# A hybrid decoder layer on one Trainium2 core: half 1's Q and T tables leave the input projection, scores change sign, key halves travel by DMA, and the down projection prepares three blocks ahead

## The chip, the cores and the metric

The kernel runs on one core of a Trainium2 chip. Its engines are TensorE (PE, with its weight loads PEld), VectorE (DVE), ScalarE (ACT), GpSimd (POOL) and SyncE (SP, which here only issues DMAs). The metric is the device time of one execution in microseconds, the median over several runs. One execution was profiled; all rows below are of that one.

## The reference

One decoder layer over 1024 tokens of width 1024. An input projection feeds two groups of heads: an S5 state-space group (32 channel groups of 16, each driving a 64-dimensional complex diagonal state) and a differential attention group (4 heads, two causal softmax maps each). Then an output projection, cross-attention over 256 memory tokens and a SwiGLU feed-forward, each with a residual and a LayerNorm. What the change touches:

```python
# S5: x_t = A x_{t-1} + B u_t, y = Re(C x) + D u, then gelu and a gate
_, _, xr, xi = lax.associative_scan(combine, (a_re, a_im, bu_re, bu_im), axis=1)
y = einsum(c_re, xr) - einsum(c_im, xi) + d * uf
y = gelu(y); y = y * sigmoid(y @ glu_w + glu_b)
...
# differential attention, per block of 128 queries
s = einsum('bqhd,bkhd->bhqk', qb, kb) * scale
s = where(dist >= 0, s + bias, -inf)
p = softmax(s, axis=-1)
attn = p[:, :, 0] - lam * p[:, :, 1]
...
# feed-forward
return (silu(gu[..., :FFN_HIDDEN]) * gu[..., FFN_HIDDEN:]) @ w_down
```

## The kernel before

**Numbers and matmuls.** All data is fp32. Most products are made as three matmuls of a rounded high part and a rest: a weight tile is loaded by SP (`wload`), then an engine rounds it (high) and subtracts (low). Where the engine is POOL, this is a TENSOR_SCALAR and a TENSOR_TENSOR of 128x1024, called a split below. Work tiles come from two pools: 47 slots `u` of 128x1024 and 6 slots `h` of 128x512. A tile takes the slot that has been free the longest, and waits until the last reader of that slot, which may be a DMA, is done. The profile drops the slot numbers: `u`, `h`, `sc`, `mm`, `tp` (the last three in PSUM) are families.

**Order.** The order on each engine is decided when the program is built: generators are woven by a planner with rough rates (`weave`), then the tile framework schedules. In the run it is fixed and each engine is in order.

**S5.** The scan runs in chunks of eight tokens. `s5_tables(hf)` builds, for half `hf` of the states, the tables in four steps: Q (DVE), T (POOL), the rotation table E (DVE) with the transposes of Q (PE, ACT), and short convolution rows `kr`: 32 matmuls, an ACT copy, a small DVE add, and DMA writes to DRAM on ACT's queue. `s5_quarter(q)` uses the tables of half `q // 2` for one quarter of the channels: SP loads the matrix M from `kr` (two DMAs), PE transposes the inputs (`Ut`) and makes v; DVE rotates v by E, runs two scans and rotates back (the rotation stage); PE sums Ut by M and the states by T; ACT and DVE make the gelu; PE transposes it; ACT writes it to DRAM (`yd`). `s5_pipe` staggers the four quarters. Beside the pipe PE has `fill`: value projection and the queries and keys of head 0.

In the kernel before, `u_proj` (the S5 input projection) is woven with `s5_tables(0)` and the first two steps of `s5_tables(1)`, Q and T; the pipe then runs the rest of `s5_tables(1)` at quarter 0.

**Attention.** `qk_proj(h + 1)` is woven with `attention(h)`. A query or key tile holds 64 channels; both 64-partition halves are filled, since the matmul takes 128 (for queries the other half holds the low part, for keys a copy). Per block and map, DVE adds the bias and takes the row maximum in one instruction, negates it (`nm`), and ACT takes the exponential with that bias.

**Down projection.** `prep(half, j)` loads block j of the weight and of the hidden activations (`hidd`, in DRAM) on SP's queue and makes high and low parts; `go` does the 24 matmuls of a block. One block is prepared ahead.

## Time and profile before

| | us |
|---|---|
| median of 3 runs (1537.68 to 1541.3) | 1539.12 |
| the profiled execution | 1539.39 |
| its span | 1537.6 |
| PE busy (share of the span) | 1424.8 (93%) |
| DVE busy | 937.7 (61%) |
| ACT busy | 528.5 (34%) |
| POOL busy | 476.7 (31%) |

The time of the profiled execution is 1.79 us longer than its span. PE is busy nearly throughout, so what a change is worth is to be looked for in the stretches where it isn't: around 120 to 200 us (the S5 pipe's start), in the attention from 280 to 480 us, and at single places later. The page also follows back the chain of work that ended last: PE 68%, DVE 13%, DMA 8%, POOL 4%, ACT 3%. All instructions are recorded under one helper line (L119, after the change L120), so rows are told apart by their tiles.

### The profile page before, as it was taken

The page shows a single profiled execution, that of the slowest core. Times are in us where ns is not written, and L with a number is a line of the kernel's source. Part 1 is how long each engine was busy: PE and PEld are TensorE (multiplying, and loading weights), DVE is VectorE, ACT ScalarE, POOL GpSimd, SP SyncE. Part 2 cuts the span into 40 slices and gives each one's busy share as a digit, 9 for nine tenths or more (in the row PEclk, how much of TensorE's full clock was granted, in tenths as well). Part 3 has the DMA queues.
Part 4 walks back from the last instruction along what each step waited for, and adds up shares of the span by engine and source line. Part 5 has one row for each costly group of instructions (what it writes and reads, how often), then busy time and mean ns, then how long its engine had stood idle before and what let it go on. Part 6 is the DMA issues. An engine that isn't in the chain of part 4 may idle for free.

```text
span 1537.6 us, 18794 instructions
## 1 busy us (share of the span) xinstructions
PE 1424.8 (93%) x7246; PEld 1202.6 (78%) x7246; DVE 937.7 (61%) x1603; ACT 528.5 (34%) x926; POOL 476.7 (31%) x382
## 2 busy tenths in 40 slices
PE   7985699999796999999999899999999998999996
PEld 6985588878676788888787677878888887888885
DVE  8893667766796555635547856656655547237405
ACT  5411233645684012424212632323323325233300
POOL 4354121022004766000155645534444420003102
PEclk9998799999998899999999999999999999999998
DMA  9104531100346224123322223322222248554501
GB/s 341 68 1 83 96 97 56 42 28 5 105 134 231 74 83 137 56 69 124 110 83 82 96 84 116 108 77 82 90 82 82 83 153 305 165 165 172 183 28 55
DMA packets 52333, 162.61 MB, mean 106 GB/s; under 512 B 5834, under 2 KB 10351, under 8 KB 52244
## 3 DMA queue, kind: packets, MB, share of 16 engines
q1 hardware_dynamic: 41652, 124.17, 24.7%
q0 software_dynamic: 7696, 26.74, 4.7%
q10 hardware_dynamic: 2896, 10.51, 2.9%
q8 instruction: 57, 0.93, 0.3%
q14 instruction: 32, 0.26, 0.1%
HBM read 126.77 MB, written 34.62 MB: 105 GB/s over the span
## 4 chain that ended last, share of the span: by engine, by line
PE 68%; DVE 13%; DMA 8%; POOL 4%; ACT 3%; issue 3%; ACTq 1%; SPq 0%; POOLq 0%; DVEq 0%
PE mm L119 35%; PE sc L119 27%; DVE u L119 9%; PE tp L119 7%; POOL u L119 3%; ACT u L119 3%; DMA u<-in_wdown_dram 1%; DMA u<-in_wgu_dram 1%; DMA u<-in_wqk_dram 1%; DMA kr<-u 1%; DMA u<-in_x_dram 1%; DMA hidd<-u 1%; DVE h L119 1%; DVE bst L119 1%; DMA u<-in_wout_dram 1%
## 5 line engine op out<-in xcount | busy, mean ns | idle before, releaser
L119 PE MATMUL mm<-u,u 128*128 128x512 f32 (+1 forms) x3288 | 727.8, 373 | 50.2 <-ACT u L119 24.0
L119 PEld LDWEIGHTS mm<-u,u 128*128 128x128 f32 x3288 | 571.7, 192 | 157.5 <-ACT u L119 26.7
L119 PE MATMUL sc<-u,u 128*128 128x512 f32 (+5 forms) x2744 | 598.9, 375 | 36.4 <-ACT u L119 30.7
L119 PEld LDWEIGHTS sc<-u,u 128*128 128x128 f32 (+2 forms) x2744 | 482.1, 199 | 124.5 <-ACT u L119 33.6
L119 DVE TENSOR_TENSOR u<-u,u 128x1024 fp32r<-128x1024 f32 (+5 forms) x257 | 314.6, 1242 | 204.9 <-ACT u L119 158.5
L119 ACT ACTIVATE u<-u 128x1024 fp32r<-128x1024 f32 (+1 forms) x200 | 195.7, 986 | 472.8 <-DMA u<-in_wgu_dram 118.5
L119 POOL TENSOR_TENSOR u<-u,u 128x512 f32<-128x512 f32 (+4 forms) x155 | 298.9, 1934 | 133.8 <-DVE u L119 90.9
L119 PE MATMUL tp<-u,u 128*128 128x512 f32 (+3 forms) x600 | 106.4, 320 | 2.4 <-ACT u L119 2.4
L119 PEld LDWEIGHTS tp<-u,u 128*128 128x128 f32 (+1 forms) x600 | 86.1, 177 | 15.8 <-ACT u L119 4.4
L119 POOL TENSOR_SCALAR bv<-bmv 128x1 f32<-128x1 f32 x24 | 7.3, 303 | 289.3 <-DVE bmv L119 289.1
L119 ACT ACTIVATE u<-mm 128x512 fp32r<-128x512 f32 (+3 forms) x84 | 47.9, 573 | 124.5 <-PE mm L119 108.8
L119 DVE TENSOR_TENSOR u<-h,u 128x512 fp32r<-128x512 f32 (+1 forms) x92 | 71.8, 800 | 17.1 <-ACT u L119 16.5
L119 POOL TENSOR_TENSOR u<-u 128x512 f32<-128x512 f32 x26 | 46.1, 1773 | 102.7 <-DMA u<-in_wgu_dram 91.5
L119 PE MATMUL tp<-eye,u 128*128 128x128 f32 x424 | 65.6, 285 | 7.2 <-DVE u L119 4.7
L119 ACT ACTIVATE u<-tp 128x512 f32<-128x512 f32 (+2 forms) x76 | 40.3, 555 | 82.1 <-PE tp L119 53.3
L119 POOL TENSOR_SCALAR u<-u 128x1024 fp32r<-128x1024 f32 x14 | 15.9, 1133 | 161.0 <-DMA u<-in_wqk_dram 80.3
L119 PEld LDWEIGHTS tp<-eye,u 128*128 128x128 f32 x424 | 52.5, 147 | 15.7 <-DVE u L119 5.0
L119 DVE SCALAR_TENSOR_TENSOR u<-u,mm 128x512 f32<-128x512 f32 x36 | 24.6, 683 | 54.1 <-PE mm L119 50.5
L119 ACT ACTIVATE u<-sc 128x512 f32<-128x512 f32 (+2 forms) x61 | 31.6, 541 | 50.8 <-PE sc L119 43.9
L119 ACT ACTIVATE u<-h 128x512 fp32r<-128x512 f32 (+1 forms) x60 | 36.1, 648 | 35.7 <-DMA h<-hidd 14.0
L119 ACT ACTIVATE h<-tp,pp 128x512 f32<-128x512 f32 x40 | 29.5, 775 | 48.2 <-PE tp L119 37.0
L119 DVE BATCH_NORM_STATS2 bst<-u 128x6 f32<-128x512 f32 x64 | 43.3, 687 | 1.3
(176 smaller groups left out, 899.7 us busy)
## 6 DMA issues: line engine op xcount, KB each, us to landing
u<-in_wgu_dram SPq DMA_DIRECT2D x52, 512.0 KB, 4.0
u<-in_wdown_dram SPq DMA_DIRECT2D x44, 512.0 KB, 4.4
h<-hidd SPq DMA_DIRECT2D x44, 256.0 KB, 4.9
u<-in_x_dram SPq DMA_DIRECT2D x16, 512.0 KB, 7.8
rd<-u POOLq DMA_DIRECT2D x16, 512.0 KB, 3.1
u<-rd SPq DMA_DIRECT2D x16, 512.0 KB, 3.6
hidd<-h POOLq DMA_DIRECT2D x22, 256.0 KB, 2.3
hidd<-u POOLq DMA_DIRECT2D x22, 256.0 KB, 3.4
```

The source lines that it names most:

```text
L119: ins = f(*args, **kw)
```

## The change

Four edits:

- **Tables.** A new function `s5_turns(hf)` holds the E step. Beside `u_proj` now run `s5_tables(0)` and only `s5_turns(1)`; Q, T, the transposes and the `kr` rows of half 1 run inside the pipe, at quarter 1.
- **Scores.** Queries and bias are scaled by -1, so the scores have the other sign. DVE's combined instruction takes a minimum instead of a maximum, and ACT's exponential reads it with scale -1. The 64 instructions `nm` fall away.
- **Keys.** The second 64-partition half of each key tile (high and low part) is copied by a DMA on POOL's queue instead of a DVE copy: 32 DMAs of 64x512 (128 KB) for 32 copies.
- **Down.** Three blocks are prepared ahead (`DD = 3`) instead of one.

DVE has 96 instructions fewer, POOL 32 more; the numbers of instructions on PE, ACT and SP are the same.

```diff
@@ -73,6 +73,7 @@
 R0 = 2
 R1 = 0.8
 PRE = 2
+DD = 3
 WPRE = 1
 T1A = 1
 R2 = 0.6
@@ -663,6 +664,23 @@
 
     tabs = {}
 
+    rots = {}
+
+    def s5_turns(hf):
+        j0 = 8 * hf
+        g8 = pv["g8"]
+        Er, Ei, Et = U([128, 8, 128]), U([128, 8, 128]), H([128, 8, 64])
+        ve.memset(Er[:, :, 0:1], 1.0)
+        ve.memset(Ei[:, :, 0:1], 0.0)
+        for l in range(7):
+            n = 1 << l
+            shp = [128, 8, n]
+            cmul(ve, Er[:, :, n:2 * n], Ei[:, :, n:2 * n], Er[:, :, 0:n], Ei[:, :, 0:n],
+                 bcv(g8[3 + l][0], shp, j0, 8), bcv(g8[3 + l][1], shp, j0, 8), Et[:, :, 0:n])
+        fr_(Et)
+        rots[hf] = (Er, Ei)
+        yield
+
     def s5_tables(hf):
         j0 = 8 * hf
         bb4, bbv, de3, pr_, pi_, pn_ = (pv[n] for n in ("bb4", "bbv", "de3", "pr", "pi", "pn"))
@@ -688,16 +706,9 @@
                  bcv(pr_[n], shp, j0, 8), bcv(pn_[n], shp, j0, 8), Tt[:, :, d, :])
         fr_(Tt)
         yield
-        g8 = pv["g8"]
-        Er, Ei, Et = U([128, 8, 128]), U([128, 8, 128]), H([128, 8, 64])
-        ve.memset(Er[:, :, 0:1], 1.0)
-        ve.memset(Ei[:, :, 0:1], 0.0)
-        for l in range(7):
-            n = 1 << l
-            shp = [128, 8, n]
-            cmul(ve, Er[:, :, n:2 * n], Ei[:, :, n:2 * n], Er[:, :, 0:n], Ei[:, :, 0:n],
-                 bcv(g8[3 + l][0], shp, j0, 8), bcv(g8[3 + l][1], shp, j0, 8), Et[:, :, 0:n])
-        fr_(Et)
+        if hf not in rots:
+            run(s5_turns(hf))
+        Er, Ei = rots[hf]
         QT = [U([128, 8, 128]) for _ in range(2)]
         for x, Q in ((0, Qr), (1, Qi)):
             for j4 in range(2):
@@ -894,13 +905,13 @@
                     hs, os_ = slice(64 * m, 64 * m + 64), slice(64 - 64 * m, 128 - 64 * m)
                     if w_ == h:
                         orv = flip(o[hs])
-                        act(blk4(Qs[m][hs, s]), orv, scale=0.125)
-                        stt(blk4(Qs[m][os_, s]), orv, 0.125, blk4(Qs[m][hs, s].bitcast(F32)), ALU.mult, ALU.subtract)
+                        act(blk4(Qs[m][hs, s]), orv, scale=-0.125)
+                        stt(blk4(Qs[m][os_, s]), orv, -0.125, blk4(Qs[m][hs, s].bitcast(F32)), ALU.mult, ALU.subtract)
                     else:
                         act(Ks[m][hs, s], o[hs])
                         lo_of(KL[m][hs, s], o[hs], Ks[m][hs, s])
-                        ve.tensor_copy(out=Ks[m][os_, s], in_=Ks[m][hs, s])
-                        ve.tensor_copy(out=KL[m][os_, s], in_=KL[m][hs, s])
+                        for t in (Ks[m], KL[m]):
+                            po.dma_start(out=t[os_, s].bitcast(F32), in_=t[hs, s].bitcast(F32))
                 if half == 1:
                     fr_(wqk.pop(w_))
                 yield
@@ -957,10 +968,10 @@
         o = SC()
         for c in range(2):
             pe.matmul(o[0:4, 512 * c:512 * c + 512], lhsT=rb, rhs=oh[:, 512 * c:512 * c + 512], start=True, stop=True)
-        act(bs, o[0:4, :])
+        act(bs, o[0:4, :], scale=-1.0)
         o = TP()
         pe.matmul(o[0:4, 0:128], lhsT=rb, rhs=oh2, start=True, stop=True)
-        act(bs2, o[0:4, 0:128])
+        act(bs2, o[0:4, 0:128], scale=-1.0)
         sc_e.dma_start(out=b_dram[:, 0:1024], in_=bs)
         sc_e.dma_start(out=b_dram[:, 1024:1152], in_=bs2)
         fr_(bs, bs2, oh, oh2)
@@ -972,7 +983,8 @@
         n = 128 * (i + 1)
         qs = slice(128 * i, 128 * i + 128)
         pt = []
-        mx, nm, l, rl = S(2, "mx"), S(2, "nm"), S(2, "l"), S(2, "rl")
+
+        mx, l, rl = S(2, "mx"), S(2, "l"), S(2, "rl")
         for m in range(2):
             if m == 0 or n > 512 or not SHARE:
                 sc = SC()
@@ -984,9 +996,8 @@
                 pe.matmul(sc[:, c:c + w], lhsT=Qs[m][:, qs], rhs=KL[m][:, c:c + w], start=False, stop=True)
             s = H() if n <= 512 and HS else U()
             ve.tensor_tensor_reduce(out=s[:, 0:n], in0=sc[:, 0:n], in1=W[:, 896 - 128 * i:1024], scale=1.0,
-                                    scalar=-3e38, op0=ALU.add, op1=ALU.max, accum_out=mx[:, m:m + 1])
-            ts(ve, nm[:, m:m + 1], mx[:, m:m + 1], -1.0, ALU.mult)
-            act(s[:, 0:n], s[:, 0:n], func=AF.Exp, bias=nm[:, m:m + 1], accum=l[:, m:m + 1])
+                                    scalar=3e38, op0=ALU.add, op1=ALU.min, accum_out=mx[:, m:m + 1])
+            act(s[:, 0:n], s[:, 0:n], func=AF.Exp, scale=-1.0, bias=mx[:, m:m + 1], accum=l[:, m:m + 1])
             pt.append(s)
         ve.reciprocal(out=rl, in_=l)
         cf = S(1, "cf")
@@ -1430,10 +1441,12 @@
                 sy.dma_start(out=out[128 * ti:128 * ti + 128, n], in_=z[:, n])
             fr_(z)
 
-        nxt = prep(0, 0)
+        ahead = [prep(0, j) for j in range(DD)]
         for half in range(2):
             for j in range(NJ - LAST):
-                (w, hx), nxt = nxt, (prep(half, j + 1) if j + 1 < NJ - LAST else None)
+                w, hx = ahead.pop(0)
+                if j + DD < NJ - LAST:
+                    ahead.append(prep(half, j + DD))
                 for i in range(4):
                     go(j, w, hx, i)
                 fr_(w, hx)
@@ -1442,7 +1455,7 @@
             zs = [load(r_dram[2][4 * half])]
             last = [prep(half, j) for j in range(NJ - LAST, NJ)]
             if half == 0:
-                nxt = prep(1, 0)
+                ahead = [prep(1, j) for j in range(DD)]
             for i in range(4):
                 ti = 4 * half + i
                 if i < 3:
@@ -1485,7 +1498,7 @@
     run(upto(mk, MS[3]))
     s5_setup()
     t1 = s5_tables(1)
-    weave((u_proj(), 1), (seq(s5_tables(0), upto(t1, 2)), R0, P1), (upto(mk, MS[4]), RM))
+    weave((u_proj(), 1), (seq(s5_tables(0), s5_turns(1)), R0, P1), (upto(mk, MS[4]), RM))
     v1 = v_proj(1)
     fill = seq(vg, qk_proj(0), upto(v1, V0))
     sq = [s5_quarter(q) for q in range(4)]
@@ -1496,7 +1509,7 @@
         next(sq[0])
         yield
         for q in range(4):
-            if q == 0:
+            if q == 1:
                 run(t1)
             if q < 3:
                 next(sq[q + 1])
```

What moves on the engines, at three places.

POOL, where the T table of half 1 stands. In the kernel before (u_1332, u_1333 and u_1334 are the T table of half 1 and its scratch; the first row is the end of half 0's):

```order
L119 TENSOR_TENSOR u_1066<-u_1066,u_1067 128x8x64
L119 TENSOR_TENSOR u_1332<-u_943,ar_825 128x8x16
L119 TENSOR_TENSOR u_1333<-u_943,an_827 128x8x16
L119 TENSOR_TENSOR u_1334<-u_943,an_827 128x8x16
L119 TENSOR_TENSOR u_1332<-u_1332,u_1334 128x8x16
L119 TENSOR_TENSOR u_1334<-u_943,ar_825 128x8x16
L119 TENSOR_TENSOR u_1332<-u_1332,ar_825 128x8x16
L119 TENSOR_TENSOR u_1333<-u_1332,an_827 128x8x16
```

After the change, the same place (u_1749 to u_1751 are now that table, u_1632 is a query weight):

```order
L120 MEMSET h_1872 128x4
L120 TENSOR_SCALAR u_1634<-u_1632 128x1024
L120 TENSOR_TENSOR u_1635<-u_1632,u_1634 128x1024
L120 TENSOR_TENSOR u_1750<-u_943,an_827 128x8x16
L120 TENSOR_TENSOR u_1749<-u_943,ar_825 128x8x16
L120 TENSOR_TENSOR u_1751<-u_943,an_827 128x8x16
L120 TENSOR_TENSOR u_1749<-u_1749,u_1751 128x8x16
```

The table no longer follows half 0's at once: it stands behind the split of the query weight, with other slots.

DVE, the rotation stage of quarter 1. In the kernel before (u_1784, u_1785 and u_1794 are the stage, u_1731 and h_1740 the gelu of quarter 0):

```order
L119 TENSOR_TENSOR u_1784<-sc_69,u_1144 128x512
L119 TENSOR_TENSOR u_1785<-sc_69,u_1145 128x512
L119 SCALAR_TENSOR_TENSOR u_1731<-h_1732,sc_70 128x8x16 x4
L119 TENSOR_TENSOR u_1784<-u_1784,u_1785 128x512 x2
L119 SCALAR_TENSOR_TENSOR u_1785<-h_1655,u_1784 128x512
L119 SCALAR_TENSOR_TENSOR h_1740<-h_1740,sc_70 128x512
L119 SCALAR_TENSOR_TENSOR u_1785<-h_1655,u_1784 128x512
L119 TENSOR_TENSOR u_1784<-u_1785,u_1144 128x4x127
L119 MEMSET u_1784 128x8
L119 TENSOR_TENSOR u_1794<-u_1785,u_1145 128x4x127
L119 SCALAR_TENSOR_TENSOR u_1731<-h_1740,sc_70 128x8x16 x4
L119 TENSOR_TENSOR u_1784<-u_1785,u_1145 128x4x127
```

After the change (u_1668, u_1669 and u_1678 are the stage, u_1726 to u_1728 the Q table of half 1, h_1616 and u_1615 the gelu of quarter 0, u_1638 a query):

```order
L120 TENSOR_TENSOR u_1668<-u_1669,u_1144 128x4x127
L120 MEMSET u_1668 128x8
L120 TENSOR_TENSOR u_1678<-u_1669,u_1145 128x4x127
L120 TENSOR_TENSOR u_1668<-u_1669,u_1145 128x4x127
L120 TENSOR_TENSOR u_1678<-u_1669,u_1144 128x4x127
L120 TENSOR_TENSOR u_1668<-u_1668,u_1678 128x4x127
L120 TENSOR_TENSOR u_1728<-u_1727,ai_826 128x8x16
L120 SCALAR_TENSOR_TENSOR h_1616<-h_1616,sc_70 128x512
L120 TENSOR_TENSOR u_1668<-u_1668,u_1678 128x4x127
L120 TENSOR_TENSOR u_1726<-u_1726,u_1728 128x8x16
L120 SCALAR_TENSOR_TENSOR u_1638<-mm_71,u_1638 64x512
L120 SCALAR_TENSOR_TENSOR u_1615<-h_1616,sc_70 128x8x16 x4
```

The Q table's instructions now stand among those of the stage and of the gelu.

SP, the down projection of half 0, with the semaphores of each row's wait. In the kernel before (the last row loads the weight of block 4):

```order
L119 DMA u_10136<-in_wdown_dram 128x1024 [waits PE_49]
L119 DMA h_10283<-hidd 128x512 [waits DMAHW1_49,DVE_49]
L119 DMA u_10171<-in_wdown_dram 128x1024 [waits DMAHW5_49,PE_49]
L119 DMA h_10318<-hidd 128x512 [waits DMAHW6_49,DVE_49]
L119 DMA u_10311<-in_wdown_dram 128x1024 [waits DMAHW7_49,PE_49]
L119 DMA h_10248<-hidd 128x512 [waits DMAHW2_49,DMAHW0_49,DVE_49]
L119 DMA h_10213<-hidd 128x512 [waits DVE_49]
L119 DMA u_10346<-in_wdown_dram 128x1024 [waits DMASW5_49,PE_49]
L119 DMA u_10381<-in_wdown_dram 128x1024 [waits DMAHW3_49,PE_49]
L119 DMA u_10031<-in_wdown_dram 128x1024 [waits DMAHW4_49,DMASW3_49]
```

After the change (the last row is again block 4's weight):

```order
L120 DMA u_10167<-in_wdown_dram 128x1024 [waits DVE_49]
L120 DMA h_9929<-hidd 128x512 [waits DMASW4_49,DVE_49]
L120 DMA u_9992<-in_wdown_dram 128x1024 [waits DMAHW5_49,PE_49]
L120 DMA u_10027<-in_wdown_dram 128x1024 [waits DMAHW6_49,PE_49]
L120 DMA h_10174<-hidd 128x512 [waits DMAHW7_49,DVE_49]
L120 DMA h_9894<-hidd 128x512 [waits DMAHW0_49,DMASW2_49]
L120 DMA h_10139<-hidd 128x512 [waits DMAHW4_49,DMAHW1_49,DVE_49]
L120 DMA h_10069<-hidd 128x512 [waits DMAHW2_49,DVE_49]
L120 DMA u_10307<-in_wdown_dram 128x1024 [waits DMAHW5_49,DMAHW3_49,DVE_49]
L120 DMA u_9887<-in_wdown_dram 128x1024 [waits DMASW3_49]
```

The loads just ahead of block 4's weight waited for PE before; now the last waits for PE are six rows further up, and the loads between wait for DVE or for DMAs.

## Rows read from the trace of the kernel before

**Rows 1.** Busy us (instructions) of PE, PEld, DVE, ACT, POOL; granted clock, DMA, GB/s.

```profile
120.00:160.00 40.00, 21.43 (x167) 19.91 (x167) 14.05 (x49) 5.77 (x12) 16.27 (x25) 0.79 0.37 74
160.00:200.00 40.00, 25.96 (x194) 21.48 (x192) 26.13 (x40) 7.90 (x14) 7.07 (x6) 0.79 0.55 106
...
280.00:480.00 200.00, 176.29 (x1056) 152.12 (x1055) 149.75 (x336) 123.35 (x299) 33.88 (x17) 0.98 0.25 80
1290.00:1320.00 30.00, 25.64 (x102) 20.62 (x101) 18.83 (x22) 13.91 (x18) 0.54 (x1) 0.89 0.74 266
```

**Rows 2.** Timeline of PE, 127 to 215 us: start, length, instruction, count, idle before.

```profile
127.42 7.19 PE L119 MATMUL mm<-u,u 128*128 128x256 f32 x58
152.94 1.12 PE L119 MATMUL sc<-u,u 128*64 128x128 f32 x8 [18.32 <-ACT u L119]
...
186.30 2.07 PE L119 MATMUL mm<-u,u 128*128 128x512 f32 x4 [10.20 <-POOL u L119]
...
207.83 6.75 PE L119 MATMUL mm<-u,u 128*128 128x512 f32 x29
```

**Rows 3.** Timeline of ACT, 116 to 153 us.

```profile
119.57 6.52 ACTq L119 DMA_DIRECT2D kr<-u  x2
...
152.28 1.08 ACT L119 ACTIVATE u<-tp 128x512 f32<-128x512 f32 x2 [17.04 <-POOL u L119]
```

**Rows 4.** Timeline of POOL, 92 to 187 us.

```profile
92.64 1.37 POOL L119 TENSOR_TENSOR u<-u,an 128x512 f32<-128x512 f32 x1
...
135.55 0.40 POOL L119 TENSOR_TENSOR u<-u,an 128x128 f32<-128x128 f32 x1 [6.24 <-DMA kr<-u]
...
150.99 1.26 POOL L119 TENSOR_TENSOR u<-u,u 128x512 f32<-128x512 f32 x1
...
185.20 1.04 POOL L119 TENSOR_SCALAR u<-u 128x1024 fp32r<-128x1024 f32 x1 [18.74 <-DMA u<-in_wqk_dram]
```

**Rows 5.** Timeline of DVE, 92 to 193 us.

```profile
93.03 1.53 DVE L119 TENSOR_TENSOR u<-u,ai 128x512 f32<-128x512 f32 x1
...
98.55 0.68 DVE L119 TENSOR_TENSOR u<-u,ai 128x512 f32<-128x512 f32 x1
...
106.38 0.42 DVE L119 TENSOR_TENSOR u<-u,h 128x256 f32<-128x256 f32 x1
...
157.46 2.49 DVE L119 TENSOR_TENSOR u<-sc,u 128x512 f32<-128x512 f32 x4 [22.96 <-PE sc L119]
...
164.63 2.46 DVE L119 TENSOR_TENSOR u<-u,u 128x508 f32<-128x508 f32 x4
...
178.54 0.87 DVE L119 SCALAR_TENSOR_TENSOR u<-h,sc 128x128 f32<-128x128 f32 x4
...
185.35 7.56 DVE L119 TENSOR_TENSOR u<-u,u 128x508 f32<-128x508 f32 x4
```

**Rows 6.** DMA issues by tile: KB each, median us from issue to landing.

```profile
hidd<-h POOLq DMA_DIRECT2D x22, 256.0 KB, 2.3
...
kr<-u ACTq DMA_DIRECT2D x8, 512.0 KB, 11.9
u<-in_wqk_dram SPq DMA_DIRECT2D x8, 512.0 KB, 3.6
...
u<-kr SPq DMA_DIRECT2D x8, 256.0 KB, 8.3
...
yd<-u ACTq DMA_DIRECT2D x4, 512.0 KB, 3.3
```

**Rows 7.** DVE by form, 200 to 480 us: busy us, mean ns, idle before.

```profile
L119 DVE CAST u<-u 64x512 fp32r<-64x512 f32 x32 | 15.4, 499 | 0.8
...
L119 DVE TENSOR_SCALAR nm<-mx 128x1 f32<-128x1 f32 x64 | 9.3, 150 | 0.6
```

**Rows 8.** Timelines of SP and PE in the down projection.

```profile
1294.75 3.90 SPq L119 DMA_DIRECT2D u<-in_wdown_dram  x3
...
1304.86 1.22 PE L119 MATMUL sc<-u,u 128*128 128x512 f32 x2 [4.37 <-ACT u L119]
```


## The prediction

> **What bounds the kernel now.** I read the busy time of the engines stretch by stretch first. PE is the engine that is nearly always busy, so I look for its idle time and ask what ended it. From 120 to 200 us it is busy for 21.43 and 25.96 of 40 us each, 32.6 us idle, at a granted clock of 0.79 on the mean; from 280 to 480 us it is idle for 23.7 of 200; from 1290 to 1320 us for 4.4 of 30, at 0.89 [rows 1]. The change touches all three stretches.
>
> In the first, two waits of PE make 28.5 of the 32.6 us [rows 2]. The 18.32 us before 152.94 end with an ACT copy, which itself waited 17.04 us for POOL [rows 3]: the copy's tile takes a scratch slot of half 1's T table, which POOL could only begin in earnest at 135.55, after DMA writes of `kr` had landed, and ended at 152.25 [rows 4]. The 10.20 us before 186.30 end with a split on POOL, which waited for a query or key weight (18.74 us of idle POOL) [rows 4]. In attention PE's idle time is spread over many short waits, with no single one to name. In the down projection one wait of 4.37 us stands out, behind ACT [rows 8].
>
> **The tables.** What goes away is the wait for POOL at 152.28. What comes is a new path, which I follow with durations of before.
>
> DVE can start the rotation stage of quarter 0 when the last `kr` write lands, for its scratch tile takes that slot: 135.5 (the write was issued in the 119.57 row, and the POOL row at 135.55 waited for the same write) [rows 3, 4]. From there to the last gelu instruction of quarter 0, which PE's next transposes need, DVE has in order: two rotation stages of 9.6 us each (157.46 to the end of the 164.63 row, 167.09), twelve instructions of the Q table of half 1 of 128x128 and 128x256 (0.2 to 0.42 each, 3.8 in all), and gelu and query work of 4.5 us (four instructions of 0.87 together, twice, and four of some 0.68) [rows 5]. 19.2 + 3.8 + 4.5 = 27.5, so 163 if nothing slows DVE.
>
> But POOL now builds the T table of half 1 just then. It waits for the query weight's split and for matmuls of PE, so it starts near 140 and takes some 17 us (16.7 from 135.55 to 152.25 with DVE idle) [rows 4]. Where both engines ran, DVE was slowed: the same 128x512 product took 1.53 us at 93.03, beside a POOL instruction, and 0.68 at 98.55, after POOL's last; the four of 128x508 took 7.56 us at 185.35 beside POOL's split, and 2.46 at 164.63 [rows 4, 5]. That is 0.44 and 0.33 of the speed; I take 0.41. Of the 17 us, 2.5 are rotation products that read PSUM and that I leave unslowed, since no row shows one of these beside POOL; of the other 14.5 DVE gets 5.9 done and loses 8.6. So PE's transposes can start at 163 + 8.6 = 171.7. The Trainium skill, GPSIMD Engine Reference, section Specifications, says that GpSimd's SBUF interface is shared with VectorE, with contention for VectorE instructions in a two-port mode or with two SBUF inputs. The slowed rows have two SBUF inputs, so the trace agrees; without that rule or these rows one would let the table hide, and the sum would be some 12 us lower (the first rival).
>
> PE gets there earlier. It has some 28.7 us of work from 126.5 on (0.124 us for a 128x256 matmul in the 127.42 row, 0.233 for a 128x512 in the 207.83 row) [rows 2] and 3 us of small waits: 158. So it idles 13.5 us. Behind these transposes ACT copies (1.1) and writes `yd` (3.3), the key weight takes that slot and loads (3.6), POOL rounds it (1.04) [rows 3, 4, 6]: 171.7 + 1.1 + 1.1 + 3.3 + 3.6 + 1.04 = 182; PE, done with other work at 179.5, idles 2.3. Then the `kr` rows of half 1: matmuls, copy and add to 187, writes 11.9, loads of M 8.3 [rows 6], so M is there at 207, and PE, with 12.2 us of work behind the matmuls, waits 7.5. Quarter 3's rotation stage costs another 4 to 5 (DVE beside POOL's splits again). With 2 us of small ones PE idles 30 to 31 us where it idled 32.6. The clock falls in both, after waits of like size. **Tables: -2 us.** Bounds: -17 if the T table does not slow DVE (8.6) and the later splits neither (4), and the small waits vanish; +9 if DVE is stopped by POOL nearly all the time (the 185.35 row lost 5.1 us to 5.4 of POOL), which adds some 5.5 to the first wait and 5 to the later stage.
>
> **Scores and keys.** Between 200 and 480 us DVE loses 64 instructions of 150 ns (9.3 us) and 32 copies of 499 ns (15.4) [rows 7], together 24.7 of the 149.75 us that it was busy from 280 on, nearly all of it there [rows 1]. `nm` also stands in the chain from the scores to the exponential, twice a block. DVE is no bound there, busy three quarters of the time, so only PE's 23.7 us of idle can be won, and part of that waits for ACT alone. I take 7, near a third: **-7 us**; bounds 0 (the waits are ACT's) and -14. Keys of head h+1 are used 71 or more matmuls after they are made, some 12 us or more; a DMA on POOL's queue landed in 2.3 us [rows 6], so I cost it at nothing. The Trainium skill's page DMA: Bandwidth & Descriptors, section SWDGE vs HWDGE vs iDMA, would send plain copies by SP or ACT, and says that VectorE can lock GpSimd out of the memory in which it writes its descriptors. It speaks for the last rival, which is the price if the cover is gone; no row here shows such a lock.
>
> **Down.** PE waited 4.37 us for the high part of block 4's weight, whose load was the third in the SP row from 1294.75 to 1298.65, held up by loads ahead that waited for PE [rows 8]. Then the clock stayed low: 25.64 us of work at 0.89 holds 2.8 us of loss [rows 1]. In the new order SP's last wait for PE ahead of it is six rows earlier; I place the issue at about 1293.4, 5 us sooner, which is just what PE lacks. 4.4 + 2.8 = 7.2, less a remainder: **-6 us**; bounds 0 and -7.
>
> **Sum.** 1539.4 (the profiled time, 0.3 above the median) - 2 - 7 - 6 = 1524.4, so 1524 against the median.
>
> **Rivals.**
> - The T table hides: POOL and DVE collide little, because POOL's instructions fall into DVE's waits. For it: DVE idled 22.96 us before its 157.46 row [rows 5]; against it: those waits go with the change. Tables -17: 1509. Chance 0.20.
> - The pipe is held longer: DVE is stopped as in the 185.35 row throughout. Tables +9 and more, the scores and keys give less since DVE is not the limit: 1538. Chance 0.14.
> - The new order does not reach PE in attention and in the down projection: the waits pass to ACT's exponentials and to the hidden loads behind block 4. For it: DVE, which is relieved, is idle a quarter of the time in attention [rows 1]. Only -2 is left: 1537. Chance 0.10.
> - Slower: keys late. The four DMAs of a head's half stand in POOL's queue behind splits that wait for weights, as the one at 185.20 did for 18.74 us [rows 4]. There are eight such groups, each needed by the scores of the next head. If PE waits 4 us in each, 32 - 15 gives 1556. It decides from (15 + 3) / 8 = 2.3 us a group. Against it: the distance of some 12 us. Chance 0.08.
>
> **How the numbers follow.** The forecast has 0.48 and, for itself, 1514 to 1533. The bound for a difference is 0.2%, 3 us, so 1536 to 1542 counts as the same. Faster: 0.48 + 0.20 + 0.04 of the second rival + 0.04 of the third = 0.76; same: 0.04 + 0.06 = 0.10; slower: 0.06 + 0.08 = 0.14. The range reaches to 1506, below which I leave 0.06 of the first rival, and to 1541, above which lie the keys and part of the second.
>
> **What would show it.** Right: no ACT wait for POOL near 152; DVE without a gap from 136 to near 172, its two-input instructions at twice their time until POOL ends near 157; one PE wait of 10 to 17 us for DVE, then one for M's load near 200; no `nm`, no CAST; PE idle from the start of attention to its end down by 4 to 10 us; no wait over 1 us at block 4. Wrong: PE's first wait ending near 163 (the first rival), `kr` writes of 16 us as those from 119.57 to 135.5, PE waiting for a DMA on POOL's queue, or a new wait in the down projection at a later block.

## The result and the profile after

| | before | after |
|---|---|---|
| median of 6 runs each, us | 1540.21 | 1529.51 |
| range, us | 1537.68 to 1546.84 | 1526.79 to 1531.42 |
| the profiled execution, us | 1539.39 | 1530.15 |
| its span, us | 1537.6 | 1528.4 |
| PE / DVE / ACT / POOL busy, us | 1424.8 / 937.7 / 528.5 / 476.7 | 1424.2 / 918.2 / 526.8 / 494.3 |

The ratio is 0.9923 (95% interval 0.9906 to 0.9939): 11.9 us, 0.8%, faster. PE's busy time is the same, so on balance the gain is PE's idle time; the two profiled spans lie 9.2 us apart. The windows of the changed kernel, which answer to [rows 1] (columns as there):

```profile
120.00:160.00 40.00, 35.83 (x265) 31.20 (x263) 27.57 (x36) 6.17 (x13) 21.67 (x24) 0.91 0.35 82
160.00:200.00 40.00, 26.45 (x225) 22.29 (x224) 20.79 (x45) 14.54 (x26) 15.08 (x15) 0.87 0.51 119
280.00:480.00 200.00, 180.57 (x1081) 154.99 (x1080) 130.46 (x257) 121.94 (x296) 40.69 (x33) 0.97 0.32 99
480.00:530.00 50.00, 38.68 (x164) 30.57 (x163) 26.34 (x28) 7.58 (x11) 34.06 (x18) 0.83 0.34 123
1290.00:1320.00 30.00, 27.92 (x123) 22.44 (x122) 19.48 (x25) 16.31 (x24) 0.00 (x0) 1.00 0.75 249
```

From 120 to 160 us PE is busy 14.4 us longer than before; from 160 to 200 it gained 0.5, and from 200 to 240, where it was never idle before, it now idles 7.6: over the three together 7.3 us less idle time. In attention it is 4.3 less, with DVE 19.3 us less busy, and 3.0 us more from 480 to 530 (41.63 busy before). In the down projection 2.3 less, at a granted clock of 1.00 instead of 0.89.

These windows are fixed in time, and the changed kernel runs ahead in them, so they do not hold the same work. Compared at the same instruction it leads the kernel before by 5.3 us at DVE's first score reduction in attention, the combined instruction (239.71 against 245.05), by 9.0 at the last of these 64 (454.45, 463.40), by 7.8 in the middle of the cross-attention scores on PE (653.31, 661.07), by 11.7 at the end of PE's last matmul (the two rows below) and by 9.2 at the end of the span. One execution can be off by some 2 us in this: the kernels with the sign, the keys or the down projection alone (below) lead the kernel before by 1.8 to 2.4 us at 220 us, before anything in their orders differs.

```profile
1518.46 6.96 PE L119 MATMUL tp<-u,u 128*128 128x512 f32 x30
1506.73 6.96 PE L120 MATMUL tp<-u,u 128*128 128x512 f32 x30
```

Behind that matmul the changed kernel takes 14.7 us to the end, the kernel before 12.2.

PE's timeline at the places of [rows 2, 8]: a first short wait for DVE, the transposes of quarter 0's gelu (170.00), the two waits for the matrix M of quarter 2, and block 4 of the down projection.

```profile
146.38 0.80 PE L120 MATMUL sc<-u,u 64*128 64x128 f32 x4 [3.80 <-DVE u L120]
170.00 1.97 PE L120 MATMUL tp<-eye,u 128*128 128x128 f32 x8 [9.91 <-DVE u L120]
201.90 0.79 PE L120 MATMUL sc<-u,u 128*128 128x128 f32 x2 [3.90 <-DMA u<-kr]
206.65 3.36 PE L120 MATMUL sc<-u,u 128*128 128x128 f32 x14 [3.96 <-DMA u<-kr]
1295.10 0.73 PE L120 MATMUL sc<-u,u 128*128 128x512 f32 x2 [1.70 <-ACT u L120]
```

SP's load of block 4's weight is the second of this row, which answers to SP's in [rows 8]:

```profile
1287.15 1.89 SPq L120 DMA_DIRECT2D u<-in_wdown_dram  x2
```

The 18.32 us behind POOL's scratch slot are gone, and of the 10.20 behind POOL's split 1.01 are left (180.04); in their place are 3.80 and 9.91 us for DVE and 7.9 for M. POOL, from the split of the query weight through half 1's T table (139.10 to the end of the 166.17 row) to the split of the key weight, answers to [rows 4]:

```profile
136.45 2.69 POOL L120 TENSOR_TENSOR u<-u,u 128x1024 fp32r<-128x1024 f32 x1
139.10 0.85 POOL L120 TENSOR_TENSOR u<-u,an 128x128 f32<-128x128 f32 x1
...
154.88 1.96 POOL L120 TENSOR_TENSOR u<-u,an 128x512 f32<-128x512 f32 x1
...
162.33 1.03 POOL L120 TENSOR_TENSOR u<-u,an 128x512 f32<-128x512 f32 x1
...
166.17 1.32 POOL L120 TENSOR_TENSOR u<-u,u 128x512 f32<-128x512 f32 x1
...
178.94 1.04 POOL L120 TENSOR_SCALAR u<-u 128x1024 fp32r<-128x1024 f32 x1 [8.11 <-DMA u<-in_wqk_dram]
```

DVE in the same time, and the same operations later without POOL (205.35, 206.55); it answers to [rows 5]:

```profile
135.75 3.94 DVE L120 TENSOR_TENSOR u<-u,u 128x512 f32<-128x512 f32 x2
...
148.24 2.47 DVE L120 TENSOR_TENSOR u<-sc,u 128x512 f32<-128x512 f32 x4
...
152.44 3.55 DVE L120 TENSOR_TENSOR_SCAN u<-h,u 128x512 f32<-128x512 f32 x2
...
169.07 0.87 DVE L120 SCALAR_TENSOR_TENSOR u<-h,sc 128x128 f32<-128x128 f32 x4
...
205.35 1.28 DVE L120 TENSOR_TENSOR u<-u,u 128x512 f32<-128x512 f32 x2
206.55 2.33 DVE L120 TENSOR_TENSOR_SCAN u<-h,u 128x512 f32<-128x512 f32 x2
```

Read them together. Two products of 1.28 us (205.35) take 3.94 beside POOL's split: 2.66 more, where the split's subtraction itself takes 2.69. The scans take 3.55 instead of 2.33 beside the T table. The products that read PSUM (`u<-sc,u`) keep their 2.47. POOL is slowed too: one form of 128x512 takes 1.96 beside DVE's two-input work (154.88) and 1.03 beside DVE's products that read PSUM (162.33). The table takes 28.4 us against 16.7 before [rows 4]; 3.8 of these are no slower work but waits for DVE, at two memsets that stand among the table's instructions. DMA issues (KB, us to landing), with the new key copies, answering to [rows 6]:

```profile
kr<-u ACTq DMA_DIRECT2D x8, 512.0 KB, 11.2
...
u<-u POOLq DMA_DIRECT2D x32, 128.0 KB, 2.3
...
u<-kr SPq DMA_DIRECT2D x8, 256.0 KB, 9.7
```

### The profile page after: what moved, and what is told of

The parts are those of the page before. It is cut to its first block, busy times and chain, and to the rows that moved or that the text cites. A ratio compares the mean times of both kernels' runs of the same rounds, so it can differ in the third digit from the quotient of the medians.

```text
span 1528.4 us, 18806 instructions
## 1 busy us (share of the span) xinstructions
PE 1424.2 (93%) x7246; PEld 1201.2 (79%) x7246; DVE 918.2 (60%) x1507; ACT 526.8 (34%) x926; POOL 494.3 (32%) x414
## 3 DMA queue, kind: packets, MB, share of 16 engines
q1 hardware_dynamic: 41652, 124.17, 24.7%
## 4 chain that ended last, share of the span: by engine, by line
PE 63%; DVE 13%; DMA 10%; issue 5%; POOL 4%; ACT 3%; SPq 0%; ACTq 0%; POOLq 0%; DVEq 0%
PE mm L120 33%; PE sc L120 23%; DVE u L120 11%; PE tp L120 7%; POOL u L120 3%; ACT u L120 3%; DMA u<-in_wgu_dram 2%; DMA kr<-u 2%; DMA u<-in_x_dram 1%; DMA u<-in_wkvv_dram 1%; DVE h L120 1%; DMA u<-kr 1%; DMA hidd<-u 1%; DMA u<-in_wqk_dram 1%; ACT h L120 1%
## 5 line engine op out<-in xcount | busy, mean ns | idle before, releaser
L120 PE MATMUL sc<-u,u 128*128 128x512 f32 (+4 forms) x2744 | 598.6, 375 | 25.6 <-DVE u L120 8.1
L120 PEld LDWEIGHTS tp<-u,u 128*128 128x128 f32 (+1 forms) x600 | 85.8, 176 | 14.4 <-ACT u L120 2.8
L120 DVE TENSOR_TENSOR u<-mm,u 128x512 fp32r<-128x512 f32 (+2 forms) x44 | 27.9, 637 | 29.7 <-ACT u L120 29.5
```

The source lines that it names most:

```text
L120: ins = f(*args, **kw)
```

## The experiments

My theory: the tables free PE from POOL's slot but put DVE's rotation stages beside POOL's table; DVE's smaller load shortens attention; three blocks bring block 4's weight in time. Rivals: the parts do nothing of their own and the gain comes from the order of PE's instructions, which each edit moves; or a part loses what another gains. Ratios are to the kernel before; that of the whole change is 0.9923.

**The four parts, each alone.** The tables:

```diff
-    weave((u_proj(), 1), (seq(s5_tables(0), upto(t1, 2)), R0, P1), ...
+    weave((u_proj(), 1), (seq(s5_tables(0), s5_turns(1)), R0, P1), ...
-            if q == 0:
+            if q == 1:
                 run(t1)
```

> The kernel before with only the tables' edit. My theory: PE's idle time between 120 and 240 us falls from 32.6 us to the 25 us that the changed kernel shows there, so some 7 us less than before in all (ratio about 0.995), and the T table on POOL still slows DVE, so PE's transposes start near 170. Rival (the table hides, the tables are the whole gain): 10 us or more less than before (0.993 or lower). Rival (the tables give nothing, the gain is elsewhere): within 2 us of before.

Measured: 1539.04, ratio 0.9986 (0.9974 to 0.9997), some 2.2 us. PE's idle time from 120 to 240 us fell as the theory said, to 23.8; the time fell by a third of the 7 us expected. The sign:

```diff
-            ts(ve, nm[:, m:m + 1], mx[:, m:m + 1], -1.0, ALU.mult)
-            act(s[:, 0:n], s[:, 0:n], func=AF.Exp, bias=nm[:, m:m + 1], ...
+            act(s[:, 0:n], s[:, 0:n], func=AF.Exp, scale=-1.0, bias=mx[:, m:m + 1], ...
```

> The kernel before with only the sign of the scores turned. My theory: 64 instructions of 150 ns less on DVE and one link less between the row maximum and the exponential give 2 to 5 us (ratio 0.997 to 0.999), in the attention from 280 to 480 us. Rival: PE's waits there are ACT's own, and nothing that the runs can tell changes (0.999 to 1.001).

Measured: 1536.20, ratio 0.9969 (0.9956 to 0.9981), some 4.8 us, as the theory had it. The keys:

```diff
-                        ve.tensor_copy(out=Ks[m][os_, s], in_=Ks[m][hs, s])
-                        ve.tensor_copy(out=KL[m][os_, s], in_=KL[m][hs, s])
+                        for t in (Ks[m], KL[m]):
+                            po.dma_start(out=t[os_, s]..., in_=t[hs, s]...)
```

> The kernel before with only the key halves moved from DVE copies to DMAs on POOL's queue. My theory: 15.4 us less on DVE gives 2 to 4 us in attention (ratio 0.997 to 0.999), and PE never waits for one of these DMAs. Rival: the DMAs come late or crowd POOL's queue, and the kernel gets slower by 1 us or more (1.001 or higher), with PE waits for POOL's DMAs.

Measured: 1544.05, ratio 1.0012 (0.9998 to 1.0025): no gain, so the theory's 2 to 4 us did not come. The down projection:

```diff
-        nxt = prep(0, 0)
+        ahead = [prep(0, j) for j in range(DD)]    # DD = 3
```

> The kernel before with only the down projection prepared three blocks ahead. My theory: the 4.37 us wait at block 4 and the low clock behind it (together 7.2 us) shrink to a wait under 2 us, so 4 to 6 us less than before (ratio 0.996 to 0.997). Rival: the time is given back in the last output tiles, which end on DVE and on the output DMAs, and 1 us or less is left (0.999 to 1).

Measured: 1534.34, ratio 0.9948 (0.9931 to 0.9965), some 8.0 us, more than the 4 to 6 expected. The four give 13.2 us together, the whole change 11.9: they add up within the noise, which is some 4 us for such a sum. With the down projection alone PE's wait at block 4 is nearly gone:

```profile
1302.12 0.73 PE L120 MATMUL sc<-u,u 128*128 128x512 f32 x2 [0.41 <-ACT u L120]
```

The attention's window (280 to 480 us, columns as above) with the tables alone:

```profile
280.00:480.00 200.00, 172.69 (x988) 145.40 (x987) 141.57 (x317) 118.05 (x287) 31.70 (x17) 0.96 0.25 79
```

with the sign alone:

```profile
280.00:480.00 200.00, 180.14 (x1043) 154.77 (x1042) 140.03 (x280) 123.69 (x298) 32.51 (x17) 0.95 0.25 82
```

and with the keys alone, and the stretch behind it:

```profile
280.00:480.00 200.00, 176.66 (x1033) 151.22 (x1032) 137.49 (x313) 120.01 (x293) 41.82 (x33) 0.97 0.29 90
480.00:530.00 50.00, 38.91 (x197) 31.90 (x196) 28.41 (x27) 13.89 (x24) 27.13 (x14) 0.83 0.44 156
```

PE was busy 176.29 us in that window before [rows 1]. With the sign alone it is busy 3.9 us longer, but at a granted clock of 0.95 instead of 0.98, and this execution's lead over the kernel before hardly grows: 2.4 us already at the first score reduction, 2.7 at PE's last matmul. That the edit gains is shown by the runs' times; where it gains, this trace doesn't show. The keys alone relieve DVE by 12.3 us and give PE 0.4, and 480 to 530 loses 2.7 (41.63 before). The tables alone idle PE 8.8 us less from 120 to 240 us, and PE is busy 3.6 less here; at the same instruction they lead by 8.5 us at the first score reduction (236.56), by 0.3 at the last (463.13) and by 0.2 at PE's last matmul. In this execution attention took back nearly all that the tables had gained ahead of it.

**The whole without the keys.** The changed kernel with DVE's copies again:

```diff
-                        for t in (Ks[m], KL[m]):
-                            po.dma_start(out=t[os_, s]..., in_=t[hs, s]...)
+                        ve.tensor_copy(out=Ks[m][os_, s], in_=Ks[m][hs, s])
+                        ve.tensor_copy(out=KL[m][os_, s], in_=KL[m][hs, s])
```

> The changed kernel with DVE copies for the second key halves again (32 copies of 64x512, no DMAs on POOL's queue for them); the other three edits stay. If the parts add up, the keys' DMAs cost some 1.8 us here too, as they did alone: the changed kernel less 1.8 us, ratio to before 0.991, and PE idle between 480 and 530 us as in the changed kernel without the keys' edit. Rival: with the sign turned, DVE is what is late, so taking its copies away is worth 3 us or more in the whole change, and this kernel comes out at 1533, ratio 0.995.

Measured: 1529.97, ratio 0.9932 (0.9915 to 0.9949): the changed kernel within its interval. Neither number came true, it lies between them: in time the keys' edit is worth nothing that the runs can tell. Neither in the changed kernel nor in that with the keys alone does PE wait for a DMA of the key halves. But the edit has a price at the very end:

| | PE's last matmul ends, us | span, us | behind it, us |
|---|---|---|---|
| before | 1525.42 | 1537.62 | 12.2 |
| the keys alone | 1523.02 | 1537.84 | 14.8 |
| the changed kernel | 1513.69 | 1528.37 | 14.7 |
| the same without the keys' edit | 1516.70 | 1528.76 | 12.1 |

All nine traces of kernels with these DMAs take 14.7 to 14.8 us behind PE's last matmul, all five without them 12.1 to 12.2. The difference lies in one place: when SP has ended its work (1522.80 in the changed kernel, 1534.67 before), all engines wait for POOL's last signal (1527.63, 1536.88). It comes 4.83 to 4.84 us after SP with the 32 DMAs on POOL's queue and 2.21 to 2.23 us after SP without. What POOL does in that time isn't shown. So the edit costs 2.6 us there, and PE seems to win some of that earlier: it ends 2.4 and 3.0 us sooner in the two pairs, of single executions that can be off by some 2 us. Whether the same copies issued by SP or ACT would keep the one without the other was not run.

**Without half 1's T table.**

```diff
+        if hf == 1:
+            po.memset(Tr, 0.0)
+            po.memset(Tn, 0.0)
+            po.memset(Tt[:, 0, 0, :], 0.0)
+        else:
             cmul(po, Tr..., Tn..., c0, n0, ...)
```

> The changed kernel without the computation of the T table of half 1: POOL fills the tile with zeros instead, so the states of half 1 are left out of the output. Order of PE and ACT unchanged. Theory (POOL's table slows DVE's two-input instructions in the rotation stages): the two scans of 3.55 us take 2.3, the 128x508 adds of 2.07 take 1.3, PE's transposes of quarter 0's gelu start at 162 to 165 instead of 170.0 and wait 2 to 5 us instead of 9.91; the whole is 5 to 8 us shorter than the changed kernel, ratio to before 0.988. Rival 1 (DVE is slow there for a reason of its own): transposes at 170 within 1 us, same time as the changed kernel. Rival 2 (the wait only moves, to the key weight's load or to the M load): transposes earlier, but less than 2 us of it left at 280 us.

Measured: 1524.29, ratio 0.9896 (0.9878 to 0.9914), some 4.2 us below the changed kernel by the ratios (0.4 to 8). Its DVE, PE and ACT at the same places:

```profile
136.17 3.86 DVE L120 TENSOR_TENSOR u<-u,u 128x512 f32<-128x512 f32 x2
139.96 2.33 DVE L120 TENSOR_TENSOR_SCAN u<-h,u 128x512 f32<-128x512 f32 x2
...
161.95 0.87 DVE L120 SCALAR_TENSOR_TENSOR u<-h,sc 128x128 f32<-128x128 f32 x4
```

```profile
162.87 1.97 PE L120 MATMUL tp<-eye,u 128*128 128x128 f32 x8 [6.93 <-DVE u L120]
...
195.41 0.57 PE L120 MATMUL sc<-u,u 128*128 128x128 f32 x2 [4.41 <-DMA u<-kr]
```

With only the table gone and the order of PE, ACT and DVE unchanged, the scans run at 2.33 and the transposes start 7.1 us sooner (in four other kernels with the table in this place they start between 169.96 and 171.32). The products beside the split, which stays, still take 3.86. So POOL's table slows DVE, as the theory said; the rival that DVE is slow by itself falls. The other rival falls too: of the 7.1 us 5.5 are left at the first score reduction and 6.1 at the end of this trace, though the waits for M are 9.3 us in all, 1.4 more than with the table. The time fell by less than the 5 to 8 us expected, but the interval reaches into that range.

**The negations behind the exponential.**

```diff
             act(s[:, 0:n], s[:, 0:n], func=AF.Exp, scale=-1.0, bias=mx[:, m:m + 1], ...
+            ts(ve, nm[:, m:m + 1], mx[:, m:m + 1], -1.0, ALU.mult)
```

> The changed kernel with the 64 negations of 128x1 put back on DVE, but written behind the exponential and read by nobody: DVE's work as before the sign was turned, the chain from scores to exponential as after. Theory (the negation cost because it stood in the chain): same as the changed kernel within 1.5 us, ratio to before 0.992. Rival (DVE's load of 9.3 us is what counts): 4 to 5 us slower than the changed kernel, ratio 0.995.

Measured: 1536.32, ratio 0.9966 (0.9948 to 0.9985): some 6.6 us slower than the changed kernel by the ratios (3 to 10), and PE's busy time in attention falls back from 180.57, at a lower granted clock (0.94 instead of 0.97):

```profile
280.00:480.00 200.00, 177.59 (x1043) 154.59 (x1042) 135.73 (x307) 119.34 (x293) 40.68 (x33) 0.94 0.32 94
```

So the negations cost as much where nobody waits for them, and my theory of the chain falls. The rival of DVE's time in the score sequence is left, and beside it that of PE's order, which differs from the changed kernel's from 273.8 us on. I then wrote as many negations among the projections:

```diff
+                if h:
+                    for c in range(6 if w_ == h and half == 0 else 5):
+                        ts(ve, nm[:, c:c + 1], pv["nlam"], -1.0, ALU.mult)
                 yield
```

> The changed kernel with 63 dummy negations of 128x1 on DVE, read by nobody, written among the query and key projections of heads 1 to 3 instead of behind the exponentials: as much more DVE work in the attention as with the negations there, at another place. Theory (what a small DVE instruction costs there hangs on its place: in the score sequence it delays the next reduction, among the projections it falls into slack, as the key copies did): same as the changed kernel within 1.5 us, ratio to before 0.992. Rival 1 (DVE's load counts wherever it stands): 4 to 7 us slower than the changed kernel, ratio 0.996. Rival 2 (the difference came from the other order of PE's instructions, which moves with any edit): anything between, with DVE's waits for PE as large as with the negations behind the exponentials.

Measured: 1531.95, ratio 0.9933 (0.9917 to 0.9948). It doesn't tell what it was made for. The group of these instructions (min, median and longest ns, first and last start):

```profile
L120 DVE TENSOR_SCALAR nmq<-nlam x63: 139/144/149, 68.0 to 74.3; 128x1 f32<-128x1 f32 x63
```

Their input was ready early, and all 63 ran at 68 to 74 us, ahead of attention. It shows only that with 9 us of DVE there quarter 0's transposes start 3.4 us later (173.38), and that the ratio moves by 0.0010, less than its interval.

**Half 1's T table at other times.** First earlier, beside the input projection:

```diff
-    weave((u_proj(), 1), (seq(s5_tables(0), s5_turns(1)), R0, P1), ...
+    weave((u_proj(), 1), (seq(s5_tables(0), s5_T(1), s5_turns(1)), R0, P1), ...
```

> The changed kernel with one step moved back: the T table of half 1 is built on POOL beside the input projection, between the tables of half 0 and the second rotation table; Q, transposes and kr rows of half 1 stay at quarter 1. Theory (the T table costs where it stands now, beside DVE's rotation stages, and cost before because its slot waited for the kr writes, which three slots fewer avoid): transposes of quarter 0's gelu at 162 to 165 as without the table, time 4 to 8 us below the changed kernel, ratio to before 0.988. Rival: the table now slows DVE's work on the second rotation table or takes again a slot that waits for the kr writes, so quarter 0 starts later: 0 to 4 us slower than the changed kernel, ratio 0.993 to 0.995.

Measured: 1543.13, ratio 1.0022 (1.0006 to 1.0038). DVE and POOL show why:

```profile
127.58 0.69 DVE L120 TENSOR_TENSOR u<-u,gi 128x8 f32<-128x8 f32 x1 [10.18 <-DMA kr<-u]
```

```profile
149.65 2.66 POOL L120 TENSOR_TENSOR u<-u,u 128x1024 fp32r<-128x1024 f32 x1 [21.39 <-issue]
```

The T table is done at 121, but now the rotation table's slot waits for the `kr` writes, and POOL's split comes late too (for what, the trace doesn't name); a memset of POOL behind it holds PE for 7.70 us. The wait of the kernel before has only changed its owner, as the rival said. That makes 9.0 us at the first score reduction; the other 5.5 of the 14.5 by which this trace is longer than the changed kernel's arise behind it, with PE in another order. Then later, when DVE has ended quarter 1's rotation stage:

```diff
+            gate[0] = S(1, "gate")
+            ve.tensor_copy(out=gate[0], in_=Wt[:, 1, 511:512])
         fr_(W2t, Xtt, dk)
...
+        if hf == 1:
+            po.tensor_copy(out=Tt[:, 0, 0, 0:1], in_=gate[0])
```

> The changed kernel in which POOL may go on with the T table of half 1 only when DVE has ended quarter 1's rotation stage (a copy of 128x1 by DVE, read by POOL ahead of the table's third instruction). Theory (the table costs by slowing that stage): the rotation stages run at their own speed, end at 157, and of the 8 us that PE's transposes were late about half comes back: they start at 165 to 167 instead of 170.0; POOL ends the table near 178 instead of 167.5, in time for the kr rows of half 1 at 184; 2 to 4 us faster than the changed kernel, ratio to before 0.990. Rival: the table now ends too late, the kr rows and M of quarter 2 with it, and PE's waits for M near 202 and 207 grow from 7.9 us in all to 12 or more: no gain, or up to 4 us slower.

Measured: 1538.28, ratio 0.9975 (0.9963 to 0.9987), 8 us slower than the changed kernel. PE:

```profile
163.78 1.97 PE L120 MATMUL tp<-eye,u 128*128 128x128 f32 x8 [7.47 <-DVE u L120]
...
211.20 0.80 PE L120 MATMUL sc<-u,u 128*128 128x128 f32 x2 [7.57 <-DMA u<-kr]
217.73 3.36 PE L120 MATMUL sc<-u,u 128*128 128x128 f32 x14 [4.46 <-DMA u<-kr]
```

The transposes come 6.2 us sooner, M 9.3 to 11.1 later: ACT's first `kr` write is issued at 191.33 instead of 184.29. Theory right on the first wait, rival right that there is no gain, though the loss is twice its 4 us. And later still, behind quarter 0's gelu:

```diff
-            ve.tensor_copy(out=gate[0], in_=Wt[:, 1, 511:512])
+            ve.tensor_copy(out=gate[0], in_=yg[:, 7, 127:128])
```

> As the kernel before this one, but POOL waits with the table for the last gelu instruction of quarter 0, so that nothing of it stands beside DVE's work on the way to PE's transposes. Theory: transposes at 163, as without the table; but the key weight's splits now stand among the table's instructions, it ends near 188 to 190, and the kr rows of half 1 come some 5 us later than in the changed kernel: PE's waits for M grow by about as much as the first one shrinks, and the time is that of the changed kernel within 3 us, ratio to before 0.992. Rival: the kr rows have slack, and the whole 5 us of the kernel without the table come back, ratio 0.989.

Measured: 1539.77, ratio 0.9985 (0.9968 to 1.0001). Transposes at 164.57, `kr` written from 195.48, M waited for 8.95 us, and 5.22 more for POOL. The rows of `kr` have no slack: both expectations were too good.

What is gained or lost ahead of attention does not pass through it unchanged once PE's order moves. Against the changed kernel the table behind quarter 1 is 14.6 us late at the first score reduction and 8.1 at the end; the table beside the input projection 9.0 and 14.5. Without the table, with PE's order the same throughout, 5.5 us stay 6.1.

**Four blocks ahead.**

```diff
-DD = 3
+DD = 4
```

> The changed kernel with four blocks of the down projection prepared ahead instead of three. Theory (block 4's weight was late because SP's queue held it behind loads that waited for PE; three blocks cure nearly all of it): the 1.70 us wait that is left at block 4 goes, 0 to 2 us faster than the changed kernel, ratio to before 0.991 to 0.992. Rival: four blocks take slots that the start of the down projection or the output rows need, and a wait of 2 us or more comes at another place.

Measured: 1541.72, ratio 0.9998 (0.9984 to 1.0012): the whole gain is gone. PE, ACT's high part of block 4's weight, and SP's load of it:

```profile
1305.49 1.22 PE L120 MATMUL sc<-u,u 128*128 128x512 f32 x2 [9.37 <-ACT u L120]
```

```profile
1304.38 1.06 ACT L120 ACTIVATE u<-u 128x1024 fp32r<-128x1024 f32 x1 [1.52 <-DMA u<-in_wdown_dram]
```

```profile
1297.19 0.33 SPq L120 DMA_DIRECT2D u<-in_wdown_dram  x1
```

The wait is where it was, twice as long as before [rows 8]: in the new order of SP's queue the load that PE needs is the 19th from `in_wdown_dram`, issued at 1297.19; in the changed kernel it is the 16th, issued by 1289.04. My theory expected no harm; the rival expected harm elsewhere, and it came at the same block.

## Why the prediction was right, and where it wasn't

1524 was forecast, with 1514 to 1533 for the likeliest case; 1529.5 came. The sum was 15 us of gain, the measurement 11.9. The number is right; of its three terms one was right as a mechanism, one by luck, and one is only half explained.

**Tables, -2: right in size, by two errors that cancel.** Alone they gave 2.2 us. The mechanism was as predicted: no wait for POOL near 152, transposes late for DVE (171.7 forecast, 170.0 measured), M at 207 (206.65) with 7.5 us of wait (7.9). DVE's way from 133.94 to the last gelu instruction took 36.0 us, and 28.5 without the table: a loss of 7.5 where 8.6 was worked out. POOL I had end near 157; it ended at 167.5, since it is slowed as well and waits for DVE twice. PE idles 25.4 us from 120 to 240, not 30 to 31: its own work lasted to 160, not 158, and the transposes came at 170.0, so that wait was 9.9 and not 13.5, and quarter 3 held it for 1.8 and not 4 to 5. With the tables alone that made a lead of 8.5 us at the first score reduction, of which attention took back nearly all, which I had not counted. That a term of 2 came out is therefore luck. Why attention gives it back is open: the edit also moves the order of PE's instructions there.

**Scores and keys, -7: the step that was mis-sized.** I took a third of PE's idle time for DVE's 24.7 us as one pool. The sign gave 4.8. The keys gave nothing: 1.8 us slower alone, 1.4 faster in the whole change, both inside the intervals. That the key DMAs themselves are hidden was right: they land in 2.3 us, and PE never waits for them. But "I cost it at nothing" was wrong: with them 2.6 us more pass behind PE's last matmul, in all nine traces, and neither the sum nor a rival had that. By the times the copies taken off DVE may then be worth 0.8 us to PE alone and 4.0 in the whole change, neither clear of the noise, and the end of the kernel takes most of it back.

DVE's busy time was the wrong measure all the same: 9.3 us in the score sequence gave 4.8 when they went and cost some 6.6 when they came back, 15.4 us of copies gave at most some 4. That 64 small instructions count for their place fits these runs; but each of these kernels also orders PE differently (from 271.9 us on with the sign alone, from 273.8 with the negations behind the exponential), so place and order are not told apart. The run meant to do that had its instructions at another place. The Trainium skill, DMA: Bandwidth & Descriptors, section SWDGE vs HWDGE vs iDMA, warns of VectorE locking GpSimd out of where it writes descriptors; no run here shows such a lock or a late key.

**Down, -6: right in mechanism, a little small.** Alone it gave 8.0 us. In the whole change a wait of 1.70 us is left, and the kernel's lead grows from 7.1 us before block 4 (1283.72 against 1290.81 for the same matmuls) to 11.7 behind it (1301.37 against 1313.10): 4.6 us, wait and clock together. I had block 4's load issued 5 us sooner. It is issued at 1288.70 against 1298.32; with the lead of 7.1 taken off, that is 2.5 us sooner, and the wait is 2.7 shorter. The lead stays 11.7 to PE's last matmul; 2.5 of it go behind that, to the keys' DMAs.

**The rivals.** The hidden T table did not come, and the kernel without the table shows the table's price: some 4 us, where that rival had 15. The pipe held throughout did not come either, though beside the split DVE is indeed held as long as the split lasts. That the new order does not reach PE did not come in the down projection; in attention it is near the truth for the keys, not for the sign. Late keys did not come.

No version beat the changed kernel with the whole computation: taking the keys' edit back is the same, all other timings of the table and four blocks are slower.

## What to carry to other kernels

Count an engine's relief only where the waiting engine stands behind it; here 9 us of small instructions in the score sequence were worth at least as much as 15 us of copies beside it, as far as these runs tell place from order. Compare two traces at the same instruction and not in the same window, and follow the lead to the end of the span: an edit can win on the way and lose behind the last matmul. Before moving a job to an idle stretch of another engine, look at who reads what it writes next (here the `kr` rows, with no slack) and at which transfer holds the slot it takes. A deeper prefetch can be worse: with one block more the queue held back the very load that was to come sooner.

## What the runs showed of the hardware

DVE and POOL hold each other up, not only DVE. Beside POOL's 128x1024 split (2.69 us) two DVE products with two SBUF inputs lose 2.66 us, all of it; beside the T table's instructions both lose, DVE's scans 3.55 for 2.33 us, POOL's 128x512 product 1.96 for 1.03. Products with one input in PSUM lose nothing (2.47 us for four beside the table, 2.49 at 157.46 in the kernel before with POOL idle), and POOL loses nothing beside them. Memsets by POOL cost DVE nothing either: in the kernel without the table three run from 139.43 to 141.33, and the two scans from 139.96 on keep 2.33. The Trainium skill, Trainium Architecture — The Big Picture, section What this means for kernel authors, calls the pair's shared port an exclusive lock, not a split of bandwidth; beside the split the trace agrees (2.66 of 2.69 us). Beside the table's shorter instructions each engine loses only a part, so the one share of 0.41 with which I worked was a rough stand-in: it gave 8.6 us where 7.5 were measured.

DMAs on POOL's queue that no engine waits for still had a price: with 32 more of them POOL's last signal came 4.83 us after SP's end instead of 2.21, where nothing covers it. Why was not tested.
